# Moving the first layer's sums of squares to GpSimd and reordering the first loads and ScalarE's table load, in a two-layer streaming encoder

## The chip, the core and the metric

The kernel runs on one core of a Trainium2 chip. The metric is the device time of one execution in microseconds (us), the median of three runs. The core has five engines: TensorE (PE in the rows; PEld is its weight load), VectorE (DVE), ScalarE (ACT), GpSimd (POOL) and SyncE (SP). Each runs its own instructions in order. Here SP only issues transfers; ScalarE issues a few as well.

## The reference

One inference step of an encoder of two layers for 384 token rows: 256 of a prompt and 8 x 16 of running streams. Each layer normalises x, multiplies it by one wide input projection, runs sparse attention, a convolution and a pooling group on slices of the result, projects back to x, and adds a gated embedding. What the change touches is the first normalisation and the first products:

```python
def _rmsnorm(x, g):
    xf = x.astype(jnp.float32)
    y = xf * lax.rsqrt(jnp.mean(xf * xf, axis=-1, keepdims=True) + EPS) * g.astype(jnp.float32)
    return y.astype(x.dtype)

z = _split_cols(_rmsnorm(x, norm_mix) @ w_in)
```

with x of (384, 2048) and w_in of (2048, 6224) in float32.

## The kernel before

x lies in 16 tiles of 128 features by 384 tokens, x0 to x15. Every matmul is made of three: each operand is split in a high part (rounded by ScalarE's copy) and a low part (the remainder, by VectorE), and high by high, high by low and low by high are added up in a bank of TensorE's result memory (function mm3, lines 245 to 247). The normalisation is taken out of the products: TensorE multiplies the unscaled x, and the rows are scaled afterwards by rb, the reciprocal root of the mean square.

Weights come in pieces of up to 128 x 1024. For each piece SP issues the load (line 103, function w_dma, three raw buffers), ScalarE makes the high part whi (line 116), VectorE the low part wlo (line 117, function w_split, four buffers). The first six pieces belong to the first step (function first_step, line 862): 3, 3, 3, 3, 2 and 2 feature tiles with 336 columns each (keys of the indexer, its weights, and values), where x is the stationary operand. For every tile k line 185 makes xh, line 186 xl, and lines 877 to 879 issue nine matmuls of 336 columns, 144 in all. Piece 0 is loaded and split in three parts of one tile each. Behind it come 46 steps of 48 matmuls each (function mstep, 128 output features, two pieces), whose results are evacuated from the middle of the next step on; there are three banks ("mm") for them and five ("sd") for all else.

At the start VectorE writes a tile of ones, TensorE runs seven warm-up matmuls on it (line 282; each shows as two instructions), ScalarE issues the loads of 16 columns of constants (line 298) and of x0 to x2 (line 288), and SP issues piece 0, x3, x4, piece 1, x5 to x7, piece 2, x8 to x15. ScalarE's first arithmetic instruction brings the load of its function table (ACT_TABLE_LOAD).

The sum of squares of layer 0 goes along with the first step: for each x ScalarE squares it (lines 202, 206) and VectorE adds the square to ss (line 207; class SumSq). When the step of 48 matmuls behind the first step has been issued, the function stats issues three column sums on TensorE (line 174), the reciprocal root (lines 162 to 167), and, half a step later, the transposes that make rb (lines 179 and 182). The evacuations of the first step and of all later ones wait for rb.

The tile selh (eight 128 x 128 selection matrices, needed in the attention of the streams, much later) is loaded by SP in one transfer (line 349) right behind the first step's loads and converted to bfloat16 by ScalarE (line 350).

The order of the instructions on each engine is not exactly that of the program: at compile time a scheduler puts ready instructions first by its own estimates of their durations, and puts semaphores where one engine needs another's result. What it made of the program before is seen in the trace.

Of the kernel before, what the change touches and what calls it, by code (L numbers as in the profile page):

```python
# [11 lines left out]
AF = mybir.ActivationFunctionType  # L12
OP = mybir.AluOpType
# [4 lines left out]
KD = 16  # L18
TP = 256
NB = 8  # L20
# [23 lines left out]
FIRST = 336  # L44
# [7 lines left out]
def hybrid_kernel(ctx, tc, I, O):  # L52
    nc = tc.nc
    V, A, G, T, S = nc.vector, nc.scalar, nc.gpsimd, nc.tensor, nc.sync
# [37 lines left out]
    def parts(i, n):  # L92

        m = FIRST if i == 0 else n
        return [slice(c, c + m) for c in range(0, n, m)]

    def w_dma(upto):
        while st["dma"] < min(upto, len(pieces)):
            i = st["dma"]
            src, n = pieces[i]  # L100
            r = wpool.tile([128, 8 * 128], F32, name="wraw", tag="wraw", bufs=RAWS)
            for c in parts(i, n):
                S.dma_start(out=r[:, c], in_=src[:, c])
            raw[i] = r
            st["dma"] += 1

# [20 lines left out]
    def w_ahead():  # L127
        i = st["use"]
        w_split(i + PARTS - 1)
        w_dma(i + PARTS - 1 + RAWS)  # L130
# [9 lines left out]
    ones = const.tile([128, 128], F32, name="ones")  # L140
    identb = const.tile([128, 128], BF16, name="identb")
    selh = const.tile([128, NB, 128], BF16, name="selh")
# [6 lines left out]
    def tmp(shape=(128, N), name="t", bufs=6, dt=F32):  # L149
        return act.tile(list(shape), dt, name=name, tag="tmp" if name == "t" else name, bufs=bufs)  # L150

    def bank(tag):
        return psum.tile([128, 512], F32, name=tag, tag=tag, bufs=3 if tag == "mm" else 5)
# [16 lines left out]
    def stats(sumsq, n, out):  # L170

        ps = bank("sd")
        for i in range(3):
            T.matmul(ps[:, i:i + 1], sumsq.t[:, 128 * i:128 * i + 128], ones[:, 0:1], start=True, stop=True)
        y = rsqrt(ps[:, 0:3], n, 3)
        yield
        ps = bank("sd")
        for i in range(3):
            T.transpose(ps[:, 128 * i:128 * i + 128], y[:, i:i + 1].to_broadcast([128, 128]), ident)
        out["col"] = y  # L180
        out["rb"] = act.tile([128, N], F32, name="rb", tag="rb", bufs=2)
        V.tensor_copy(out["rb"], ps[:, :N])
# [9 lines left out]
    class SumSq:  # L192
# [3 lines left out]
            self.n = 0  # L196
            self.t = None

        def add(self, x, q=None):
            if self.t is None:  # L200
                self.t = act.tile([128, N], F32, name="ss", tag="ss", bufs=2)
                A.activation(self.t, x, AF.Square)
            else:
                if q is None:
                    q = tmp()
                A.activation(q, x, AF.Square)
                V.tensor_tensor(self.t, self.t, q, OP.add)

    def buf(which, part, k, name, dt=F32R):

        return act.tile([128, N], dt, name=name, tag=f"{which}{part}{k}", bufs=1)
# [28 lines left out]
    def run_pending(gate):  # L240
        while pending and gate():
            pending.popleft()()
# [6 lines left out]
    def mstep(xs, evac, gate, c0=0):  # L249

        ps = bank("mm")
        for h in range(2):
            w_ahead()
            hi, lo = w_next()
            for j in range(8):
                k = 8 * h + j
                mm3(ps[:, :N - c0], hi[:, 128 * j:128 * j + 128], lo[:, 128 * j:128 * j + 128], xs[k][0][:, c0:],
                    xs[k][1][:, c0:], k == 0, k == KD - 1)
            if h == 0:
                run_pending(gate)  # L260
            pump()
        pending.append(lambda: evac(ps))
# [15 lines left out]
    V.memset(ones, 1.0)  # L278

    warm = bank("sd")  # L280
    for _ in range(7):
        T.matmul(warm[:, :128], ones, ones, start=True, stop=True)
    xs, xt = [], []
    ss = SumSq()

    def x_in(k):
        x = buf("B", "hl"[k // 8], k % 8, f"x{k}", F32)
        (A if k < 3 else S).dma_start(out=x, in_=I["xT"][k])
        xt.append(x)

    def x_split(k):
# [3 lines left out]
        xs.append((hi, lo))  # L295

    x_dram = dram.tile([KD, 128, N], F32, name="x_dram")
    A.dma_start(out=cst[:, 384:400], in_=I["cst"][:, 384:400])
    for k in range(3):
        x_in(k)  # L300
    w_dma(1)
    for k in range(3, KD):
        x_in(k)
        if k in (4, 7):
            w_dma(2 if k == 4 else 3)

    def square_gen():
        for k in range(KD):
            q = buf("B", "hl"[k % 2], 8 + k // 2 % 2, f"sq{k}", F32)
            ss.add(xt[k], q)  # L310
            if k % 2:
                yield

    tracks.append(Track(square_gen()))


    for l in range(DEPTH):
# [4 lines left out]
        with ExitStack() as mixctx:  # L322
            mix = mixctx.enter_context(tc.tile_pool(name=f"mix{l}", bufs=1))

            def mt(shape, tag, bufs=1, dt=F32, name=None):
                return mix.tile(list(shape), dt, name=name or tag, tag=tag, bufs=bufs)
# [3 lines left out]
            def load_tab(i):  # L330
                tabs[i] = mt([128, 2, N], "tab", name=f"tab{i}")
                S.dma_start(out=tabs[i], in_=I["tab"][i])
# [7 lines left out]
            def loads():  # L340
                if l == 0:
                    S.dma_start(out=cst[:, 400:], in_=I["cst"][:, 400:])
                    S.dma_start(out=cst[:, :384], in_=I["cst"][:, :384])
                    V.tensor_copy(identb, ident)
                load_tab(0)
                S.dma_start(out=tabt, in_=I["tabt"])
                if l == 0:
                    t = mt([128, NB, 128], "qas", name="selhf")
                    S.dma_start(out=t, in_=I["selh"])
                    A.activation(selh, t, AF.Copy)  # L350

            if l > 0:
                loads()
# [5 lines left out]
            qas = mt([128, NB, 8, TS], "qas")  # L359
            q = [buf(oth, "l", 8 + h, f"q{l}_{h}", F32) for h in range(8)]  # L360
# [70 lines left out]
            def pre_ga(m):  # L431
                if m >= 2:
                    drain(lambda: f"conv{m - 2}" in flags)
                u = mt([128, 24, HALO + TS], "up", bufs=2, name="u")
                G.memset(u[:, 0, 0:30], 0.0)
                G.memset(u[:, 1, 0:14], 0.0)
                S.dma_start(out=u[:, 16:].rearrange("p b j -> p (b j)"), in_=I["cstate"][l, m])
                u_t[m] = u
# [473 lines left out]
            def pool_mm():  # L912
                hi, lo = w_next()
                for g in range(4):
                    ps = bank("sd")
                    c = slice(128 * g, 128 * g + 128)
                    mm3(ps[:, :N], hi[:, c], lo[:, c], r_t[g][0], r_t[g][1], True, True)
                    po[g] = buf(oth, "l", g, f"po{l}_{g}", F32)
                    A.activation(po[g], ps[:, :N], AF.Copy)

            def conv_mm():
                drain(lambda: "convy" in flags)
                w_ahead()
                a = w_next()
                b = w_next()
                ys = R["ys"]
                oc = []
                for m in range(4):
                    ps = bank("sd")
                    for k in range(4):  # L930
                        hi, lo = (a, b)[m // 2]
                        j = (4 * (m % 2) + k) * 128
                        mm3(ps[:, :N], hi[:, j:j + 128], lo[:, j:j + 128], ys[k][0], ys[k][1], k == 0, k == 3)
                    o = buf(oth, "l", 4 + m, f"oc{l}_{m}", F32)
                    A.activation(o, ps[:, :N], AF.Copy)
                    oc.append(o)
                R["oc"] = oc
# [7 lines left out]
            stat_track = stats(ss, D, R)  # L945
            first_step()
            if l == 0:
                loads()
            for n, (kind, i) in enumerate(ORDER):
                if n == POOL_AT:  # L950
                    pool_mm()
                if n == CONV_AT:
                    conv_mm()
                if kind == "ga":
                    pre_ga(i)
                mstep(xs, evs[kind](i), gate, CHUNK if kind == "qi" else 0)
                if l == 0 and n == 0:
                    next(stat_track)
                    tracks.append(Track(stat_track))
            run_pending(gate)  # L960


        with ExitStack() as xctx:
            xp = xctx.enter_context(tc.tile_pool(name=f"x{l}", bufs=1))
            x = []
            for k in range(KD):
                t = xp.tile([128, N], F32, name=f"xr{l}_{k}", tag=f"xr{k}")
# [4 lines left out]
            for k in range(2):  # L972
                t = tmp()
                S.dma_start(out=t, in_=I["pT"][l, :, k])
                split(t, phi[k], plo[k])
            ss = SumSq()
# [19 lines left out]
            stat_track = stats(ss, D, R2)  # L996
# [161 lines left out]
            ss = ss2  # L1158
# [136 lines left out]
```

## Time and profile before

| | us |
|---|---|
| median of three runs | 1503.79 |
| lowest, highest run | 1502.68, 1504.21 |
| the profiled execution's own time | 1504.57 |
| its span, first to last instruction | 1502.8 |
| TensorE busy | 1482.3 |
| VectorE busy | 981.7 |
| ScalarE busy | 666.9 |
| GpSimd busy | 6.4 |

The span starts with the first instruction of any engine; times in the rows count from there. "Busy" is the time in which an engine's instructions were under way. TensorE's matmuls overlap one another, so the distance between two starts, not the duration of one, tells its pace. "x14" behind an entry says how many instructions it holds, and the arrow in brackets says how long the engine was idle before it and what it waited for. The granted clock is 1.00 at 2.4 GHz and 0.50 at 1.2 GHz.

### The profile page before, as it was taken

The numbers are of one execution on the slowest core, as the hardware profiler recorded it, in microseconds if no ns is written. First come the engines' busy times: TensorE is split into PE (matmuls) and PEld (weight loads), VectorE is DVE, ScalarE is ACT, GpSimd is POOL, SyncE is SP. The second block draws the span as 40 slices with busy tenths as digits, with TensorE's granted clock in tenths as the row PEclk, the third lists the DMA queues.
The fourth block names the chain that finished last, engine by engine and source line by source line (L and its number), as shares of the span: only waits on it lengthen the run. The fifth ranks groups of instructions, "written<-read, shape, count | busy, mean of one in ns | idle before, by whom it ended". The sixth has DMA issues, their size and how long they took to land.

```text
span 1502.8 us, 22679 instructions
## 1 busy us (share of the span) xinstructions
PE 1482.3 (99%) x8832; PEld 1448.8 (96%) x8832; DVE 981.7 (65%) x1768; ACT 666.9 (44%) x1170; POOL 6.4 (0%) x40
## 2 busy tenths in 40 slices
PE   8999999999999999999999999999999999999996
PEld 8999999999999999999999999999999999999996
DVE  6778987975565444555549699978646554445554
ACT  7553424465443333444445433344644333345443
POOL 0000000000000000000000000000000000000000
PEclk9999999999999999999999999999999999999998
DMA  8554444334464444444454445443345444444332
GB/s 289 158 157 129 139 134 130 116 99 126 137 200 137 126 126 127 142 147 148 137 181 157 145 122 160 121 132 111 100 133 177 153 137 126 127 130 126 127 113 84
DMA packets 81435, 209.14 MB, mean 139 GB/s; under 512 B 11696, under 2 KB 37040, under 8 KB 81328
## 3 DMA queue, kind: packets, MB, share of 16 engines
q1 hardware_dynamic: 80464, 206.58, 44.1%
q8 instruction: 69, 1.13, 0.3%
q10 hardware_dynamic: 864, 1.12, 0.2%
q14 instruction: 38, 0.31, 0.1%
HBM read 196.90 MB, written 10.77 MB: 138 GB/s over the span
## 4 chain that ended last, share of the span: by engine, by line
PE 97%; DMA 1%; DVE 1%; ACT 0%; SPq 0%; issue 0%; DVEq 0%
PE mm L245 29%; PE mm L247 28%; PE mm L246 28%; PE sd L245 1%; PE sd L247 1%; PE sd L246 1%; PE sd L878 1%; PE sd L879 1%; PE sd L739 1%; PE sd L877 1%; PE sd L766 1%; DMA x<-in_xT_dram 1%; PE sd L672 1%; PE sd L709 1%; PE sd L801 0%; PE sd L827 0%
## 5 line engine op out<-in xcount | busy, mean ns | idle before, releaser
L116 ACT ACTIVATE whi<-wraw 128x1024 fp32r<-128x1024 f32 (+3 forms) x340 | 356.2, 1048 | 584.8 <-PE mm L246 420.7
L117 DVE TENSOR_TENSOR wlo<-wraw,whi 128x1024 fp32r<-128x1024 f32 (+3 forms) x340 | 411.0, 1209 | 228.5 <-ACT whi L116 223.3
L245 PE MATMUL mm<-xh,whi 128*128 128x384 f32 (+1 forms) x736 | 245.9, 334 | 0.0
L245 PE MATMUL mm<-nh,whi 128*128 128x384 f32 (+1 forms) x736 | 245.8, 334 | 0.0
L247 PE MATMUL mm<-nh,wlo 128*128 128x384 f32 (+1 forms) x736 | 244.8, 333 | 0.0
L247 PE MATMUL mm<-xh,wlo 128*128 128x384 f32 (+1 forms) x736 | 244.8, 333 | 0.0
L246 PE MATMUL mm<-nl,whi 128*128 128x384 f32 (+1 forms) x736 | 243.8, 331 | 0.0
L246 PE MATMUL mm<-xl,whi 128*128 128x384 f32 (+1 forms) x736 | 243.8, 331 | 0.0
L246 PE MATMUL mm<-cl,whi 128*128 128x384 f32 x512 | 171.0, 334 | 0.0
L247 PE MATMUL mm<-ch,wlo 128*128 128x384 f32 x512 | 171.0, 334 | 0.0
L245 PE MATMUL mm<-ch,whi 128*128 128x384 f32 x512 | 170.7, 334 | 0.0
L245 PE MATMUL mm<-ph,whi 128*128 128x384 f32 (+1 forms) x512 | 169.8, 332 | 0.0
L246 PE MATMUL mm<-pl,whi 128*128 128x384 f32 (+1 forms) x512 | 169.4, 331 | 0.0
L247 PE MATMUL mm<-ph,wlo 128*128 128x384 f32 (+1 forms) x512 | 169.4, 331 | 0.0
L468 DVE SCALAR_TENSOR_TENSOR ca<-u,cst,ca 128x384 f32<-128x384 f32 x240 | 146.9, 612 | 2.5
L245 PEld LDWEIGHTS mm<-xh,whi 128*128 128x128 f32 x736 | 138.2, 188 | 3.1 <-issue 1.8
L245 PEld LDWEIGHTS mm<-nh,whi 128*128 128x128 f32 x736 | 138.2, 188 | 3.1 <-issue 1.8
L247 PEld LDWEIGHTS mm<-xh,wlo 128*128 128x128 f32 x736 | 138.2, 188 | 1.6 <-issue 1.2
L247 PEld LDWEIGHTS mm<-nh,wlo 128*128 128x128 f32 x736 | 138.2, 188 | 1.6 <-issue 1.2
L246 PEld LDWEIGHTS mm<-xl,whi 128*128 128x128 f32 x736 | 138.2, 188 | 1.5 <-issue 1.0
L246 PEld LDWEIGHTS mm<-nl,whi 128*128 128x128 f32 x736 | 138.2, 188 | 1.5 <-issue 1.0
L246 PEld LDWEIGHTS mm<-pl,whi 128*128 128x128 f32 x512 | 96.2, 188 | 0.0
(274 smaller groups left out, 1877.0 us busy)
## 6 DMA issues: line engine op xcount, KB each, us to landing
wraw<-in_win_dram SPq DMA_DIRECT2D x184, 512.0 KB, 3.6
wraw<-in_wout_dram SPq DMA_DIRECT2D x64, 512.0 KB, 3.5
wraw<-in_wple_dram SPq DMA_DIRECT2D x64, 512.0 KB, 3.5
wraw<-in_wpp_dram SPq DMA_DIRECT2D x8, 512.0 KB, 3.5
wraw<-in_wfirst_dram SPq DMA_DIRECT2D x7, 504.0 KB, 3.8
xr<-in_xT_dram SPq DMA_DIRECT2D x16, 192.0 KB, 5.3
x_dram<-xr SPq DMA_DIRECT2D x16, 192.0 KB, 3.2
xr<-x_dram SPq DMA_DIRECT2D x16, 192.0 KB, 4.9
```

The source lines that it names most:

```text
L116: A.activation(hi[:, c], r[:, c], AF.Copy)
L117: V.tensor_tensor(lo[:, c], r[:, c], hi[:, c].bitcast(F32), OP.subtract)
L245: T.matmul(ps, hi_w, hx, start=first, stop=False)
L246: T.matmul(ps, hi_w, lx, start=False, stop=False)
L247: T.matmul(ps, lo_w, hx, start=False, stop=last)
L468: V.scalar_tensor_tensor(av, u[:, :, j:j + 16], w, av, OP.mult, OP.add)
L672: T.matmul(ps[j][:, :nk], qi[t + i][h, 64:192], kiT[h, :nk], start=True, stop=True)
L709: T.matmul(ps[j][:, :KS], qis[h, b + i].rearrange("p t j -> p (t j)"), kbs[i][h], start=True, stop=True)
L739: T.matmul(o, q[2 * hp + i][:, 128 * qt:128 * qt + 128], kT[g][:, :nk], start=True, stop=False)
L766: T.matmul(ps.rearrange("p (i c) -> p i c", i=4), Vt[:, kt, 128 * g:128 * g + 128], pt[:, kt], start=(kt == 0), stop=(kt == qt))
L877: T.matmul(outs[i], xh[:, c], wh, start=(k == 0), stop=False)
L878: T.matmul(outs[i], xh[:, c], wl, start=False, stop=False)
```

## The change

The diff has four parts. For layer 0 the squares of x0 to x11 and all additions to ss are made by GpSimd; the squares of x12 to x15 stay with ScalarE. ScalarE issues x0 first, then the 16 columns of constants, and then copies one column of the ones into column 128 of the bank that the warm-up matmuls write; there are eight of these instead of seven. x1, x2 and x3 are issued by SP, each behind one of the three parts of piece 0. selh is loaded and converted behind the fifth step of 48 matmuls, in two halves. Last, the column sums of layer 0 are no longer issued at the end of the first step of 48, but when the list of side tracks is stepped in the middle of the next one, and the transposes for rb at its end.

```diff
@@ -94,13 +94,15 @@
         m = FIRST if i == 0 else n
         return [slice(c, c + m) for c in range(0, n, m)]
 
-    def w_dma(upto):
+    def w_dma(upto, also=None):
         while st["dma"] < min(upto, len(pieces)):
             i = st["dma"]
             src, n = pieces[i]
             r = wpool.tile([128, 8 * 128], F32, name="wraw", tag="wraw", bufs=RAWS)
             for c in parts(i, n):
                 S.dma_start(out=r[:, c], in_=src[:, c])
+                if also is not None:
+                    also(c.start)
             raw[i] = r
             st["dma"] += 1
 
@@ -196,15 +198,22 @@
             self.n = 0
             self.t = None
 
-        def add(self, x, q=None):
+        def add(self, x, q=None, eng=None, sq=False):
+
+            def square(out):
+                if not sq:
+                    A.activation(out, x, AF.Square)
+                else:
+                    eng.tensor_tensor(out, x, x, OP.mult)
+
             if self.t is None:
                 self.t = act.tile([128, N], F32, name="ss", tag="ss", bufs=2)
-                A.activation(self.t, x, AF.Square)
+                square(self.t)
             else:
                 if q is None:
                     q = tmp()
-                A.activation(q, x, AF.Square)
-                V.tensor_tensor(self.t, self.t, q, OP.add)
+                square(q)
+                (eng or V).tensor_tensor(self.t, self.t, q, OP.add)
 
     def buf(which, part, k, name, dt=F32R):
 
@@ -278,14 +287,14 @@
     V.memset(ones, 1.0)
 
     warm = bank("sd")
-    for _ in range(7):
+    for _ in range(8):
         T.matmul(warm[:, :128], ones, ones, start=True, stop=True)
     xs, xt = [], []
     ss = SumSq()
 
     def x_in(k):
         x = buf("B", "hl"[k // 8], k % 8, f"x{k}", F32)
-        (A if k < 3 else S).dma_start(out=x, in_=I["xT"][k])
+        (A if k == 0 else S).dma_start(out=x, in_=I["xT"][k])
         xt.append(x)
 
     def x_split(k):
@@ -295,11 +304,11 @@
         xs.append((hi, lo))
 
     x_dram = dram.tile([KD, 128, N], F32, name="x_dram")
+    x_in(0)
     A.dma_start(out=cst[:, 384:400], in_=I["cst"][:, 384:400])
-    for k in range(3):
-        x_in(k)
-    w_dma(1)
-    for k in range(3, KD):
+    A.activation(warm[:, 128:129], ones[:, 0:1], AF.Copy)
+    w_dma(1, lambda c: x_in(c // FIRST + 1))
+    for k in range(4, KD):
         x_in(k)
         if k in (4, 7):
             w_dma(2 if k == 4 else 3)
@@ -307,7 +316,7 @@
     def square_gen():
         for k in range(KD):
             q = buf("B", "hl"[k % 2], 8 + k // 2 % 2, f"sq{k}", F32)
-            ss.add(xt[k], q)
+            ss.add(xt[k], q, G, k < 12)
             if k % 2:
                 yield
 
@@ -344,10 +353,6 @@
                     V.tensor_copy(identb, ident)
                 load_tab(0)
                 S.dma_start(out=tabt, in_=I["tabt"])
-                if l == 0:
-                    t = mt([128, NB, 128], "qas", name="selhf")
-                    S.dma_start(out=t, in_=I["selh"])
-                    A.activation(selh, t, AF.Copy)
 
             if l > 0:
                 loads()
@@ -955,8 +960,12 @@
                     pre_ga(i)
                 mstep(xs, evs[kind](i), gate, CHUNK if kind == "qi" else 0)
                 if l == 0 and n == 0:
-                    next(stat_track)
                     tracks.append(Track(stat_track))
+                if l == 0 and n == 4:
+                    for i in range(2):
+                        t = mt([128, 4, 128], "rp", bufs=2, name="selhf")
+                        S.dma_start(out=t, in_=I["selh"][:, 4 * i:4 * i + 4])
+                        A.activation(selh[:, 4 * i:4 * i + 4], t, AF.Copy)
             run_pending(gate)
```

## Rows read from the trace of the kernel before

**Rows 1.** The page's busy shares: us, share of the span, instructions

```profile
PE 1482.3 (99%) x8832; PEld 1448.8 (96%) x8832; DVE 981.7 (65%) x1768; ACT 666.9 (44%) x1170; POOL 6.4 (0%) x40
```

**Rows 2.** TensorE's waits over the span: line, releaser, us, times, longest

```profile
PE sd L877 <- ACT whi L116: 3.5, 2, 3.3
PE sd L878 <- DVE wlo L117: 1.8, 2, 1.5
```

**Rows 3.** Windows: stretch, length, busy us by engine, granted clock, DMA share, GB/s

```profile
7.70:12.62 4.92, 4.92 (x17) 4.92 (x18) 4.54 (x10) 4.92 (x12) 0.00 (x0) 1.00 1.04 380
12.62:23.40 10.78, 10.34 (x65) 9.79 (x64) 10.68 (x21) 10.78 (x21) 0.00 (x0) 1.00 1.06 384
23.40:26.36 2.96, 1.46 (x7) 1.17 (x8) 2.96 (x6) 2.96 (x6) 0.00 (x0) 1.00 0.27 82
26.36:29.72 3.36, 3.36 (x14) 3.36 (x13) 3.29 (x6) 1.94 (x4) 0.00 (x0) 0.50 0.89 272
```

**Rows 4.** Timeline of the beginning, ScalarE and SP: start, us, what; idle before

```profile
1.18 1.42 ACTq L288 DMA_DIRECT2D x<-in_xT_dram  x3
3.65 0.43 SPq L103 DMA_DIRECT2D wraw<-in_wfirst_dram  x1
5.36 1.28 ACT L185 ACT_TABLE_LOAD   x1 [5.36 <-DMA x<-in_xT_dram]
6.66 0.61 ACT L185 ACTIVATE xh<-x,cst 128x384 fp32r<-128x384 f32 x1
```

**Rows 5.** Timeline of TensorE in the first 37 us

```profile
1.05 3.36 PE L282 MATMUL sd<-ones 128*128 128x128 f32 x14 [1.05 <-DVE ones L278]
7.70 1.21 PE L877 MATMUL sd<-whi,xh 128*128 128x336 f32 x3 [3.29 <-ACT whi L116]
8.98 0.48 PE L879 MATMUL sd<-whi,xl 128*128 128x336 f32 x1
9.26 0.48 PE L878 MATMUL sd<-wlo,xh 128*128 128x336 f32 x1
...
26.64 0.48 PE L877 MATMUL sd<-whi,xh 128*128 128x336 f32 x1
26.92 0.48 PE L878 MATMUL sd<-wlo,xh 128*128 128x336 f32 x1
...
36.51 0.33 PE L245 MATMUL mm<-xh,whi 128*128 128x384 f32 x1
```

**Rows 6.** Groups of the first 37 us: line, shapes, count, busy us, mean ns

```profile
L186 DVE SCALAR_TENSOR_TENSOR xl<-x,cst,xh 128x384 fp32r<-128x384 f32 x16 | 9.4, 611 | 6.7 <-ACT xh L185 6.7
L207 DVE TENSOR_TENSOR ss<-ss,sq 128x384 f32<-128x384 f32 x15 | 8.3, 552 | 0.3
L206 ACT ACTIVATE sq<-x 128x384 f32<-128x384 f32 x15 | 7.6, 512 | 0.1
L117 DVE TENSOR_TENSOR wlo<-wraw,whi 128x1008 fp32r<-128x1008 f32 x3 | 3.6, 1199 | 0.0
```

**Rows 7.** Line 820: ns min/median/max, and what its engine sat idle for

```profile
L820 ACT ACTIVATE t<-sd x16: 269/277/278, 366.2 to 1146.6; 128x128 f32<-128x128 f32 x16
...
  PE sd L818: 17.8, 14
```

**Rows 8.** Line 1133, GpSimd's only arithmetic: ns min/median/max

```profile
L1133 POOL TENSOR_TENSOR xr<-xr,rbA x4: 724/727/732, 1488.9 to 1490.9; 128x256 f32<-128x256 f32 x4
```

**Rows 9.** Timeline from 44 to 53 us: column sums and scale row

```profile
44.83 0.72 PE L174 MATMUL sd<-ones,ss 128*128 128x1 f32 x6
...
52.03 0.55 DVE L182 COPY rb<-sd 128x384 f32<-128x384 f32 x1
```

**Rows 10.** Landings of weight pieces in the first 30 us

```profile
DMA to landing us min/median/max: 2.4/4.5/5.5
...
wraw<-in_wfirst_dram SPq DMA_DIRECT2D x3, 504.0 KB, 5.4
```

**Rows 11.** ScalarE's timeline near 25 us

```profile
25.14 1.05 ACT L350 ACTIVATE selh<-selhf 128x1024 bf16<-128x1024 f32 x1
```

## Prediction

> **What bounds the kernel now.** I read the page's busy shares first, then TensorE's waits, then the windows of the first 30 us, and last the order of events on each engine there. TensorE is busy in 99% of the span [rows 1], so nothing that only unloads another engine matters unless TensorE waited for it. Two lines account for its waits, but for the one ahead of the warm-ups, and all of them lie at the beginning [rows 2]: 3.3 us until the first converted weights came from ScalarE, and 1.5 us (and one short one) for a weight remainder from VectorE. From 36.5 us on it has work without a gap until the tail, which the change does not touch. So all that can be gained lies ahead of 36.5 us, where the first step (144 matmuls of 336 columns, lines 877 to 879) ends and the first matmul of the next step starts [rows 5].
>
> How long must that step take? Pairs of neighbouring starts give the pitch. At 8.98 and 9.26 us it is 0.28 us, and again at 26.64 and 26.92 us, where the clock column reads 0.50 [rows 3, 5]: that is 336 columns at 1.2 GHz. In between, from 12.62 to 23.40 us, 65 matmuls took 10.34 us, 0.159 each: 2.4 GHz. The clock column reads 1.00 in the first stage too, but the pitch says half. The 144 matmuls at 0.159 would take 22.9 us; from 7.70 to 36.51 us they took 28.8. The 5.9 us too many are the half clock at the start, the stall from 23.4 to 26.36 us (1.46 us busy in 2.96, with ScalarE and VectorE busy throughout [rows 3]), and the half clock behind the stall.
>
> **The change part by part.**
>
> *Start.* ScalarE now waits for x0, issued at 1.18 us and landed by 5.36, then loads its table for 1.28 us, then makes xh0 at 6.66, and TensorE starts at 7.70, 1.04 us behind xh0's start [rows 4, 5]. x0 moves to the slot 0.45 us earlier; with the same 4.18 us it lands at 4.9, and with the shortest landing of a first weight part, 2.4 us [rows 10], at 3.1. The table load moves off this path if it starts by 3.6 us. The copy that brings it writes one column of the bank that the warm-up matmuls write. Does it wait for them? The nearest row is a copy at line 820, which reads columns 0 to 127 of a bank and still waits for the later matmul at line 818, which writes columns 128 to 255 [rows 7]; so I take it that the copy waits for the last warm-up. 14 warm-up instructions took 3.36 us from 1.05 us on [rows 5]; 16 end at 4.9. I take the table load itself as running ahead of that wait and 0.2 us for a copy of one column (128 columns take 0.28 [rows 7]): xh0 at 5.1, TensorE at 6.15, a gain of 1.55 us. Bounds: 0.25 (table load behind the wait too: 4.9 + 1.28 + 0.2 = 6.4 instead of 6.66) and 2.8 (no wait and x0 at 3.1, where TensorE itself ends the warm-ups only at 4.9). The eighth warm-up matmul costs nothing as long as TensorE starts after 4.9. x1 and x2 go from ScalarE's queue to SP's and push piece 1 back by two issues, 0.9 us; the part on what is late next pays for that.
>
> *Clock at the start.* About 18 matmuls ran at 0.28 instead of 0.155: 2.2 us lost. The clock rose at 12.6 us, 4.9 us after the stream began and after a hole of 3.3 us behind the warm-ups. The hole would be 1.25 us. How much sooner the clock rises no row shows: between 0 and 2.2 us; I take 1.0.
>
> *Squares and sums on GpSimd.* ScalarE loses 12 squares of 0.51 us, 6.1 us, and VectorE 15 adds of 0.55, 8.3 us [rows 6]; ScalarE also loses the 1.05 us conversion at 25.14 us [rows 11]. In the 20 us in which both ran without a pause that is a third of their work, while the missing remainder came 1.5 us late. So the waits at 15.1, 23.4 and 25.6 us go, 2.0 us (1.8 on VectorE, 3.5 less 3.3 on ScalarE [rows 2]); lower bound 1.0. With the stall goes the fall of the clock behind it: 3.36 us at half clock is 1.5 us lost [rows 3]; lower bound 0.5, if a shorter stall comes back elsewhere. GpSimd gets 27 operations (12 squares, 15 adds). Its only row is a median of 0.727 us for 256 columns [rows 8]; for 384 that makes 1.09 by the columns, 0.73 if they counted for nothing: 27 of them are 29.4 or 19.7 us, and I take the 29.4. Begun at 4.9, the sum is ready at 34.3 us at most. Who needs it? The column sums at line 174, in TensorE's own order, at 44.83 us now [rows 9]; the change moves them half a step back. A step took 44.83 - 36.51 = 8.3 us, so that is 4.2 us. With a first step ended at about 31.5, they stand at 31.5 + 8.3 + 4.2 = 44 us: 10 us of slack, if GpSimd runs freely. The scale row rb, copied at 52.03 us now [rows 9], comes 4.2 us later in the order; the evacuations that wait for it free TensorE's three banks. TensorE waits nowhere behind it now [rows 2], so I cost this at 0; how much cover is left no row tells, and if it runs out, up to 4.2 us come on top, inside the range.
>
> *What is late next.* Weights: piece 1 was issued at 3.65 us [rows 4], in the new order near 4.5, and lands 5.4 us later [rows 10], at 9.9; with its conversion TensorE has it at 11. Its first 27 matmuls end between 10.3 (full clock) and 13.7 (half). I charge 1.0 us, bounds 0 and 2.0. The transfers ran at 380 GB/s all through that stretch [rows 3]; the constant selh (512 KB, 1.3 us of them) leaves it, which is why I charge no more. Its two halves, loaded and converted behind the fifth step, I cost at 0: from 26 us on TensorE waits for no conversion [rows 2].
>
> Sum: 1.55 + 1.0 + 2.0 + 1.5 - 1.0 = 5.05 us. The profiled execution took 1504.57 us, 1.77 more than its span; 1504.57 - 5.05 = 1499.5. The median of the runs lies 0.8 us below the profiled one, so 1503.8 - 5.05 gives **1498.8 us**. All upper ends give 8.5 us (2.8 + 2.2 + 2.0 + 1.5), 1495.3; all lower ones (0.25 + 0 + 1.0 + 0.5 - 2.0) give 1504.
>
> **The rivals.**
>
> *A, slower: GpSimd and VectorE shut each other out.* Nowhere in the trace does a GpSimd operation that reads SBUF run beside a VectorE operation with two SBUF inputs: in the tail, beside the four of [rows 8], VectorE reads one input from PSUM. In the first step nearly all of VectorE's work (lines 186 and 117) has two SBUF inputs, so this case is open. If only one of the two can run at a time, the work queues up: 29.4 us of GpSimd, 9.4 us of line 186, 16 x 336 columns at 1.2 us per 1008 of line 117, 6.4 us [rows 6], and some four later remainders of 1.2 us, 4.9 us, together 50 us from 4.9 on, so ready at 55 us. The sums are due at 44. Either TensorE stands 11 us at line 174, or it starves by as much in the first step: 1498.8 + 11 = 1510 us. It decides once GpSimd is held up by more than the 10 us of slack. For it: 15.8 us of VectorE's first step are of this kind. Against it: nothing that the trace shows.
> The Trainium skill states such a rule in "SBUF — State Buffer", section "SBUF: two separate sides": a VectorE operation with two SBUF inputs and a GpSimd operation that reads SBUF take a common pair of ports in turn, and the loser waits for the whole instruction. By that rule the time would be that of A; no run here shows it yet.
>
> *B, no difference: the start does not move and supply takes the rest.* The table load sits behind the warm-ups (gain 0.25), the clock rises no sooner, and the weights, which came at 380 GB/s already, hold TensorE where ScalarE and VectorE did: 0.25 + 2.0 + 1.5 - 2.0 = 1.8, 1502 us. For it: [rows 7] and the DMA column; against it: from 23.4 to 26.36 us the transfers nearly stopped (82 GB/s), so supply was not what held TensorE then.
>
> **How the numbers follow.** The forecast, gains of 3 us and more: 0.52. B: 0.14. A: 0.34; no row contradicts it and it would eat all gains. A change of under 0.2% (3 us) can hardly be told from none here. Faster by over 0.2% (below 1500.8) 0.52, within 0.14, slower (above 1506.8) 0.34. The likeliest case's own range is 1495.3 to 1501. The range that should hold 8 in 10 takes in B and most of A: 1496 to 1511.5.
>
> **What would show it.** Right: TensorE's first matmul near 6.2 us with the table load ahead of it, no wait at line 878 in the first step, no half clock near 27 us, the next step starting near 31.5 us, line 174 unwaited. A would show as GpSimd operations well above 1.1 us apart, VectorE's 0.61 and 1.20 us grown, and a wait at line 174 or 878. B would show as a first matmul near 7.4 us and ScalarE waiting for DMA on pieces 1 to 3. I am wrong if GpSimd's chain ends after 44 us.

## The result and the profile after

The median after is 1511.86 us (1510.99 to 1512.35) against 1503.24 us of the kernel before beside it: a ratio of 1.0058, 95% interval 1.0047 to 1.0070, so 8.6 us slower. The profiled execution took 1511.61 us, with a span of 1509.7 us, 6.9 us longer than before. The spans differ by less than the medians because the profiled execution of before, 1504.57 us, lies 1.3 us above its median; sums below that set one trace against the other account for the 7 us, not for the 8.6.

The page's span and busy shares, the lines that answer to [rows 1]:

```profile
span 1509.7 us, 22681 instructions
PE 1484.1 (98%) x8834; PEld 1450.5 (96%) x8834; DVE 989.5 (66%) x1753; ACT 662.9 (44%) x1160; POOL 41.0 (3%) x67
```

VectorE lost 15 additions (8.3 us by [rows 6]) and is busy 7.8 us longer. TensorE's waits (line, releaser, us, times, longest), answering to [rows 2]:

```profile
PE sd L883 <- DVE wlo L119: 9.7, 3, 6.7
PE sd L291 <- DVE ones L287: 1.1, 1, 1.1
PE sd L882 <- ACT xh L187: 0.8, 1, 0.8
```

(The second is the wait for the tile of ones ahead of the warm-ups; it was there before.) The 3.3 us ahead of the first matmul are 0.8 now, and nothing waits for whi. But the waits for a remainder, 1.8 us before, are 9.7. Line 883 is line 878 of before, 119 is 117, 188 is 186. TensorE's timeline (start, length, what; in brackets the idle time before it and what ended it), answering to [rows 5]:

```profile
1.05 3.78 PE L291 MATMUL sd<-ones 128*128 128x128 f32 x16 [1.05 <-DVE ones L287]
5.65 0.65 PE L882 MATMUL sd<-whi,xh 128*128 128x336 f32 x1 [0.81 <-ACT xh L187]
...
15.40 0.42 PE L883 MATMUL sd<-wlo,xh 128*128 128x336 f32 x1 [2.67 <-DVE wlo L119]
...
32.24 0.65 PE L883 MATMUL sd<-wlo,xh 128*128 128x336 f32 x1 [6.72 <-DVE wlo L119]
...
43.51 0.33 PE L254 MATMUL mm<-xh,whi 128*128 128x384 f32 x1
```

The first matmul starts 2.05 us sooner than before, the next step 7.0 us later. That is the difference of the spans, so all of the loss between the two profiled executions lies in the first step. The windows show what stood there (stretch, length, busy us by engine, granted clock, DMA share, GB/s), as [rows 3] do for before:

```profile
13.20:15.40 2.20, 0.00 (x1) 0.00 (x1) 2.20 (x3) 2.13 (x4) 2.20 (x2) 1.00 1.08 373
15.40:19.00 3.60, 3.60 (x15) 3.60 (x16) 3.60 (x4) 3.36 (x7) 3.60 (x4) 0.61 1.00 336
...
25.00:30.40 5.40, 0.53 (x4) 0.25 (x2) 5.40 (x6) 1.77 (x3) 5.32 (x6) 0.95 0.25 73
30.40:34.00 3.60, 1.76 (x6) 1.76 (x7) 3.60 (x3) 0.53 (x2) 3.44 (x3) 0.50 0.22 41
```

From 25.0 to 30.4 us TensorE (first column) has half a microsecond of work, ScalarE (fourth) a third of the time, the transfers move 73 GB/s, and VectorE and GpSimd (third and fifth) are busy with hardly a pause. Behind the stalls the clock column reads 0.61 and 0.50 (0.50 is 1.2 GHz).

The groups of the first 60 us (line, shapes, count, then busy us, mean ns of one, and idle before), answering to [rows 6]:

```profile
L216 POOL TENSOR_TENSOR ss<-ss,sq 128x384 f32<-128x384 f32 x15 | 20.9, 1390 | 0.5
L188 DVE SCALAR_TENSOR_TENSOR xl<-x,cst,xh 128x384 fp32r<-128x384 f32 x16 | 18.8, 1228 | 0.2 <-ACT xh L187 0.2
L207 POOL TENSOR_TENSOR sq<-x 128x384 f32<-128x384 f32 x11 | 13.6, 1238 | 0.1
L119 DVE TENSOR_TENSOR wlo<-wraw,whi 128x1008 fp32r<-128x1008 f32 x3 | 6.0, 2002 | 0.0
L353 DVE CAST identb<-cst 128x128 bf16<-128x128 f32 x1 | 1.0, 1024 | 0.0
L207 POOL TENSOR_TENSOR ss<-x 128x384 f32<-128x384 f32 x1 | 0.8, 825 | 3.1 <-DMA x<-in_xT_dram 3.1
```

The same xl took 611 ns before and takes 1228, the same remainder of 1008 columns 1199 and now 2002 [rows 6]. GpSimd's first square, made while VectorE had nothing to do, took 825 ns; the other squares and the additions took 1238 and 1390. VectorE's instructions are longer by 0.6 to 0.8 us, about one of GpSimd's. VectorE's and GpSimd's timelines around the long stall show it one by one:

```profile
20.69 9.58 DVE L188 SCALAR_TENSOR_TENSOR xl<-x,cst,xh 128x384 fp32r<-128x384 f32 x8
30.19 3.56 DVE L119 TENSOR_TENSOR wlo<-wraw,whi 128x1008 fp32r<-128x1008 f32 x2
...
22.70 1.14 POOL L207 TENSOR_TENSOR sq<-x 128x384 f32<-128x384 f32 x1
23.80 1.33 POOL L216 TENSOR_TENSOR ss<-ss,sq 128x384 f32<-128x384 f32 x1
...
28.55 10.84 POOL L216 TENSOR_TENSOR ss<-ss,sq 128x384 f32<-128x384 f32 x7
```

Eight xl take 9.58 us, 1.2 each, and GpSimd's instructions start 1.1 and 1.3 us apart: one of the one, one of the other. The fourth piece's remainder stands behind those eight on VectorE, starts at 30.19 us and frees TensorE at 32.24. Its high part had been ready since 19.64 us (18.60 + 1.04), as ScalarE's timeline shows together with the start:

```profile
1.66 1.28 ACT L118 ACT_TABLE_LOAD   x1 [1.66 <-PEq L1275]
4.00 0.48 ACT L118 ACTIVATE whi<-wraw 128x336 fp32r<-128x336 f32 x1 [1.06 <-DMA wraw<-in_wfirst_dram]
4.98 1.12 ACT L187 ACTIVATE xh<-x,cst 128x384 fp32r<-128x384 f32 x2 [0.50 <-DMA cst<-in_cst_dram]
...
6.38 0.15 ACT L309 ACTIVATE sd<-ones 128x1 f32<-128x1 f32 x1
...
18.60 1.04 ACT L118 ACTIVATE whi<-wraw 128x1008 fp32r<-128x1008 f32 x1 [0.24 <-DMA wraw<-in_wfirst_dram]
```

The result of GpSimd's chain itself, the sum, is ready at 39.4 us (28.55 + 10.84), and the column sums that need it stand at 55.99 us in TensorE's order and wait for nothing.

### The profile page after: what moved, and what is told of

Same layout as the page of the kernel before. It is cut to its first block, busy times and chain, and to the rows that moved or that the text cites. A ratio compares the mean times of both kernels' runs of the same rounds, so it can differ in the third digit from the quotient of the medians.

```text
span 1509.7 us, 22681 instructions
## 1 busy us (share of the span) xinstructions
PE 1484.1 (98%) x8834; PEld 1450.5 (96%) x8834; DVE 989.5 (66%) x1753; ACT 662.9 (44%) x1160; POOL 41.0 (3%) x67
## 4 chain that ended last, share of the span: by engine, by line
PE 97%; DVE 1%; DMA 1%; ACT 0%; SPq 0%; issue 0%; DVEq 0%; ACTq 0%
PE mm L254 28%; PE mm L256 28%; PE mm L255 28%; PE sd L254 1%; PE sd L256 1%; PE sd L255 1%; PE sd L883 1%; PE sd L884 1%; DMA wraw<-in_wfirst_dram 1%; PE sd L744 1%; PE sd L882 1%; PE sd L771 1%; PE sd L677 1%; DVE xl L188 1%; PE sd L714 1%; PE sd L806 0%
## 5 line engine op out<-in xcount | busy, mean ns | idle before, releaser
L119 DVE TENSOR_TENSOR wlo<-wraw,whi 128x1024 fp32r<-128x1024 f32 (+3 forms) x340 | 416.5, 1225 | 233.5 <-ACT whi L118 231.2
```

The lines of the kernel that those rows point to most:

```text
L119: V.tensor_tensor(lo[:, c], r[:, c], hi[:, c].bitcast(F32), OP.subtract)
```

## The experiments

The theory behind the first runs was Rival A: GpSimd's operations lengthen VectorE's, and the remainders come late. Against it stood that the new order of VectorE's instructions is to blame (the fourth remainder behind eight xl), or the other three parts of the change. The trace of before answers part of this by itself: there, too, the fourth remainder stood behind eight xl, of 0.6 us each:

```profile
19.08 1.67 DVE L186 SCALAR_TENSOR_TENSOR xl<-x,cst,xh 128x384 fp32r<-128x384 f32 x3
...
21.14 1.14 DVE L186 SCALAR_TENSOR_TENSOR xl<-x,cst,xh 128x384 fp32r<-128x384 f32 x2
...
22.33 0.61 DVE L186 SCALAR_TENSOR_TENSOR xl<-x,cst,xh 128x384 fp32r<-128x384 f32 x1
...
23.33 1.14 DVE L186 SCALAR_TENSOR_TENSOR xl<-x,cst,xh 128x384 fp32r<-128x384 f32 x2
24.39 1.20 DVE L117 TENSOR_TENSOR wlo<-wraw,whi 128x1008 fp32r<-128x1008 f32 x1
```

So that place in the queue is not new, and the expectations that call it so are wrong in this.

Every time is given with its ratio to the kernel before, timed on the same chip, and the ratio's 95% interval; a difference between two experiments can be one between two chips. The line numbers of one and the same instruction differ by a few from run to run; the names of the tiles are the same.

**The change without GpSimd's part.** The sums come back to ScalarE and VectorE, all else as changed.

```diff
-            ss.add(xt[k], q, G, k < 12)
+            ss.add(xt[k], q)
```

> The changed kernel with its squares back on ScalarE and its sums back on VectorE; the other three parts of the change stay, and behind the first step TensorE's order is the same. Exclusion theory (a VectorE operation with two SBUF inputs and a GpSimd operation that reads SBUF run one after the other): line 188 falls from 1.23 back to 0.61 us and the 1008-column remainder from 2.00 to 1.20; the waits at line 883 (9.7 us now) fall under 4 us; 1498 to 1503 us. Order theory (the remainder of the fourth piece is queued behind eight xl now, and the loads come later, whatever GpSimd does): this order is kept, so the wait of 6.7 us stays and the time is 1508 to 1512.

Measured: 1502.98 us against 1502.81, ratio 0.9999 (0.999 to 1.0008). The 8.6 us are gone. The fourth remainder still comes behind the same eight xl, so that order alone does not cost them; TensorE's waits for remainders are 1.2 us instead of 9.7. The groups:

```profile
L188 DVE SCALAR_TENSOR_TENSOR xl<-x,cst,xh 128x384 fp32r<-128x384 f32 x16 | 9.5, 616 | 0.0
L119 DVE TENSOR_TENSOR wlo<-wraw,whi 128x1008 fp32r<-128x1008 f32 x3 | 3.6, 1206 | 0.5 <-ACT whi L118 0.5
```

VectorE's durations are those of before. The first matmul starts at 5.79 us, 1.9 us sooner than before, but TensorE then waits 1.3 us at 22.04 and 1.2 us at 24.01 with half clock behind it: the other parts together are worth nothing that this measurement tells from none as long as the sums are made in the first step.

**GpSimd's part alone.** The kernel before, with only the squares and additions on GpSimd.

```diff
...
-            ss.add(xt[k], q)
+            ss.add(xt[k], q, G, k < 12)
```

> The kernel before with only the squares and sums moved to GpSimd; loads, table load, warm-ups and selh as before. Exclusion theory: VectorE's two-input operations double as in the changed kernel, TensorE waits 8 us or more for remainders, 1509 to 1515 us (worse than the changed kernel, as the earlier start is missing). Order theory: with the loads in their old order 1502 to 1504.

Measured: 1513.89 us, ratio 1.0073 (1.0056 to 1.0089), 11.1 us slower than before. The waits:

```profile
PE sd L885 <- DVE wlo L117: 9.3, 3, 6.7
PE sd L884 <- ACT whi L116: 3.3, 1, 3.3
```

The same long wait of 6.7 us, beside the old start of 3.3; xl took 1209 ns and the 1008-column remainder 2000. So the part that costs is this one, with the old loads and the old start too.

**No sums at all.** The squares and sums of x1 to x15 are left out, on every engine.

```diff
-            q = buf("B", "hl"[k % 2], 8 + k // 2 % 2, f"sq{k}", F32)
-            ss.add(xt[k], q, G, k < 12)
+            q = None
+            if k == 0:
+                ss.add(xt[k], q)
```

> The changed kernel without the sum of squares of x1 to x15 (the scale rows come from x0 alone): neither GpSimd nor ScalarE nor VectorE makes them. Exclusion theory: this is the case that the forecast's sum described, VectorE at 0.61 and 1.20 us, no wait over 1 us at line 883, 1496 to 1499 us. Order theory: 1506 or more, as the eight xl are still queued ahead of the fourth remainder.

Measured: 1499.27 us, ratio 0.9974 (0.9964 to 0.9983): 3.5 us faster than before. This is close to the prediction's own case, sums that disturb nobody. TensorE's only wait behind the warm-ups, and the window from the clock's rise to the end of the first step:

```profile
PE sd L883 <- ACT xh L187: 0.7, 1, 0.7
```

```profile
12.06:31.99 19.93, 19.93 (x130) 19.91 (x130) 13.12 (x23) 10.71 (x18) 0.00 (x0) 1.00 0.82 298
```

No stall and no half clock behind one; the next step starts at 31.99 us, where 31.5 was forecast. The order changed too: the six column-sum instructions ran at 7.42 us, inside the first step, and up to 12.06 us the matmuls ran at a pitch of 0.28 us, 1.2 GHz.

**Half the columns.** GpSimd's operations take 192 of the 384 columns, but for the first; the rest of the sum is left out.

```diff
...
-                    eng.tensor_tensor(out, x, x, OP.mult)
+                    m = N if out is self.t else n
+                    eng.tensor_tensor(out[:, :m], x[:, :m], x[:, :m], OP.mult)
...
-                (eng or V).tensor_tensor(self.t, self.t, q, OP.add)
+                (eng or V).tensor_tensor(self.t[:, :n], self.t[:, :n], q[:, :n], OP.add)
...
```

> The changed kernel with GpSimd's operations (all but the first square) on 192 of the 384 columns; the rest of the sum is left out. Their number and order stay. Exclusion theory: a VectorE operation waits for one GpSimd operation of half the length, line 188 near 0.90 to 1.0 us instead of 1.23, TensorE's waits at line 883 about half of 9.7 us, 1502 to 1507 us. If the number of GpSimd's instructions or their semaphores were what slows VectorE, line 188 stays at 1.2 us and the time at 1511 to 1513.

Measured: 1509.04 us, ratio 1.004 (1.0025 to 1.0055). The durations answered to the number of columns:

```profile
L189 DVE SCALAR_TENSOR_TENSOR xl<-x,cst,xh 128x384 fp32r<-128x384 f32 x16 | 13.3, 882 | 0.1
L120 DVE TENSOR_TENSOR wlo<-wraw,whi 128x1008 fp32r<-128x1008 f32 x3 | 4.3, 1437 | 1.6 <-ACT whi L119 1.6
```

xl is 0.27 us above its own 0.611, where whole columns put 0.62 on it. The time was missed (1502 to 1507 expected). The order had changed: the column sums moved into the first step, to 28.35 us, and the waits are others.

```profile
PE sd L884 <- ACT whi L119: 3.5, 1, 3.5
PE sd L177 <- POOL ss L218: 2.4, 1, 2.4
```

The second is the other form of Rival A, TensorE standing at the column sums (line 174 of before) for GpSimd's chain. So this run shows that VectorE's durations follow the length of GpSimd's operations, and nothing on how the time goes with it.

**GpSimd busy without reading.** The sums left out as above, and 64 memsets of 384 columns that nobody reads.

```diff
-            ss.add(xt[k], q, G, k < 12)
+            for _ in range(4):
+                G.memset(q, 0.0)
+            if k == 0:
+                ss.add(xt[k])
```

> The kernel of e3 (no sums but x0's) with 64 memsets of 128 x 384 on GpSimd that nobody reads: GpSimd is busy for some 25 to 30 us of the beginning, but it reads nothing from SBUF. If only a GpSimd operation that reads SBUF shuts VectorE out: line 188 stays at 0.61 us and the time at e3's, 1498 to 1500.5. If any GpSimd operation on SBUF does: line 188 near 1.0 us or more and 1504 or more.

Measured: 1499.62 us, ratio 0.9971 (0.996 to 0.9982), as without the memsets. They filled GpSimd until 23.9 us:

```profile
L320 POOL MEMSET sq<- 128x384 f32 x64 | 22.9, 416 | 0.3 <-POOLq L1278 0.3
L188 DVE SCALAR_TENSOR_TENSOR xl<-x,cst,xh 128x384 fp32r<-128x384 f32 x16 | 8.9, 609 | 0.5 <-ACT xh L187 0.5
```

A GpSimd busy with writing alone does not lengthen VectorE's two-input operations; one busy with the squares and additions, which read two operands from SBUF, does. No run has a GpSimd operation with one operand.

**Only the additions on GpSimd.** All squares on ScalarE.

```diff
-            ss.add(xt[k], q, G, k < 12)
+            ss.add(xt[k], q, G)
```

> The changed kernel with all squares on ScalarE; only the 15 sums are GpSimd's. TensorE's order is that of the changed kernel. Exclusion theory: 15 instead of 27 GpSimd operations stand in VectorE's way in the first step; each takes 0.6 us or so from VectorE, so some 7 of the 16 us come back, TensorE's waits at line 883 fall from 9.7 to 2 to 5 us, 1503 to 1508 us. If only the length of GpSimd's chain mattered: no wait at the column sums before, so no change, 1511 to 1513.

Measured: 1509.90 us, ratio 1.0043 (1.0028 to 1.0058): a miss. With 15 instead of 27 operations the longest wait for a remainder was 6.3 us instead of 6.7. VectorE's and GpSimd's timelines tell why:

```profile
19.05 9.04 DVE L188 SCALAR_TENSOR_TENSOR xl<-x,cst,xh 128x384 fp32r<-128x384 f32 x7
...
12.65 15.03 POOL L216 TENSOR_TENSOR ss<-ss,sq 128x384 f32<-128x384 f32 x11 [0.88 <-ACT sq L205]
```

Eleven additions, once they no longer had to wait for ScalarE's squares, ran without a pause from 12.65 to 27.68 us, and so beside seven of the eight xl that stand ahead of the fourth remainder, 1.29 us each. Here it counted less how many operations GpSimd had than beside which of VectorE's they fell. The additions read ss and sq, not x, so it is not the reading of one and the same tile that lengthens xl.

**The fourth remainder ahead of the last four xl.** GpSimd's work unchanged; xl12 to xl15 are put behind the fourth piece's remainder.

```diff
...
+        if k >= 12:
+            with tc.issue_after(st["fourth"]):
+                split_scaled(xt[k], vec(0, NM + k), hi, lo)
...
```

> The changed kernel with one order more: VectorE makes the remainder of the fourth weight piece ahead of xl12 to xl15 instead of behind them; all of GpSimd's work stays. If exclusion costs its time through what is queued ahead of that remainder: four xl of 1.2 us come out of the 6.7 us wait, which falls to 2 us or so (a later wait of 1 to 2 us for xl12 or the fifth remainder may appear), and the half clock behind it may go, 1505 to 1508 us. If VectorE's lost 16 us have to be paid wherever they lie, the wait only moves: 1510 to 1512.

Measured: 1507.16 us, ratio 1.0024 (1.0014 to 1.0034). The waits for remainders fell from 9.7 to 6.4 us, with the longest 2.7:

```profile
PE sd L889 <- DVE wlo L119: 6.4, 4, 2.7
```

The place in VectorE's queue made some 4.7 of the lost microseconds (1511.86 - 1507.16, on two chips); the rest, 4.2 us against the kernel before on the same chip (1502.92), is still there, and xl still takes 1240 ns. The whole loss needs both: instructions that have become twice as long, which is new, and an order, as it was before, that puts eight of them ahead of an urgent one.

**The sums behind the first step's splits.** No GpSimd; squares and additions on ScalarE and VectorE, but placed behind the split of the first step's last piece.

```diff
...
-            ss.add(xt[k], q, G, k < 12)
-            if k % 2:
+            a, v = st["behind"]
+            with tc.issue_after(a), tc.issue_after(v):
+                ss.add(xt[k], q)
+            if k in (5, 11):
...
```

> The changed kernel, complete, without GpSimd: ScalarE squares, VectorE adds, but all of them ordered behind the split of the first step's last weight piece. Exclusion theory: the first step runs as in the kernel without sums (next step starts near 32 us, no wait over 1 us), and ScalarE and VectorE have idle time for 8 us of sums each behind it: 1498 to 1500.5 us, faster than the kernel before. If the sums only move the stall: a wait of 2 us or more at lines 245 to 247 or at the column sums, 1501.5 to 1505.

Measured: 1498.66 us, ratio 0.997 (0.9959 to 0.9981), faster than both kernels. The next step starts at 30.61 us. Its waits:

```profile
PE sd L885 <- ACT whi L118: 1.7, 1, 1.7
...
PE sd L886 <- DVE wlo L119: 0.5, 1, 0.5
```

What the change wanted, the sums out of the first step's way, was to be had by moving them in time instead of to another engine. The 1.7 and 0.5 us end at 11.74 and 12.98 us; they are for piece 1 of the weights, on which ScalarE could begin at 10.64 us.

**The same with the beginning of before.** The kernel before, its sums and column sums placed as in the last one.

```diff
...
-            ss.add(xt[k], q)
-            if k % 2:
+            a, v = st["behind"]
+            with tc.issue_after(a), tc.issue_after(v):
+                ss.add(xt[k], q)
+            if k in (5, 11):
...
-                    next(stat_track)
```

> The kernel before (old order of loads, table load behind x0, selh early, seven warm-ups) with its sums on ScalarE and VectorE ordered behind the split of the first step's last piece and the column sums half a step later, as in e5. What it differs by from e5 is the new beginning alone: first matmul near 7.7 instead of 5.6 us. If the beginning is worth what it starts earlier: 1500 to 1501.5 us, 2 us above e5's 1498.7. If transfers set the pace of the first step: 1498.5 to 1499.5, as e5.

Measured: 1499.86 us, ratio 0.9977 (0.9968 to 0.9987), with the first matmul at 6.94 us and the next step at 31.75. The later sums alone are worth 3.1 us (1502.92 - 1499.86); with the new beginning and the later load of selh, by which the two kernels differ too, it is 4.4 (1503.10 - 1498.66). The rest, 1.2 us (1499.86 - 1498.66), lies between what the two theories expected, on two chips; I don't call it settled. With the same order of loads as before, x0 was awaited until 4.61 us here and until 5.36 in the trace of before [rows 4], so that part of an earlier first matmul can be the spread of single executions.

**No copy.** The kernel without GpSimd's part, without the copy into the warm-up bank and with seven warm-up matmuls.

```diff
-    for _ in range(8):
+    for _ in range(7):
...
-    A.activation(warm[:, 128:129], ones[:, 0:1], AF.Copy)
...
-            ss.add(xt[k], q, G, k < 12)
+            ss.add(xt[k], q)
```

> The kernel of e1 (changed, sums on ScalarE and VectorE) without the copy of a constant and with seven warm-ups instead of eight. If the copy brings the table load forward, the load falls back behind the wait for x0 and TensorE's first matmul comes at 6.5 us or later, 1503.5 to 1506. If the new order of the first instructions brings it (ScalarE's first one waits for one transfer only), the load stays at 1.7 us, the first matmul near 5.8, and the time at 1501.5 to 1504.5, the same as e1.

Measured: 1502.44 us, ratio 0.9996 (0.9987 to 1.0005), against 0.9999 with the copy. ScalarE's timeline:

```profile
1.66 1.28 ACT L118 ACT_TABLE_LOAD   x1 [1.66 <-PEq L1274]
```

The table load comes at the same time without the copy, ahead of the first conversion of weights (line 118), and the first matmul at 5.78 us, against 5.79. The copy brings nothing here.

**The loads of x1 to x3 in ScalarE's queue.** The kernel with the later sums, and three loads moved back from SP's queue.

```diff
-        (A if k == 0 else S).dma_start(out=x, in_=I["xT"][k])
+        (A if k < 4 else S).dma_start(out=x, in_=I["xT"][k])
```

> The kernel with the sums on ScalarE and VectorE behind the first step's splits, but with the loads of x1, x2 and x3 in ScalarE's queue behind x0's and the constant's, as x1 and x2 were before, instead of SyncE's. It asks what the term on supply in the prediction (1.0 us, bounds 0 and 2.0) was worth: with the three loads out of SyncE's queue, piece 1 of the weights is issued 1.4 us sooner (4.57 to about 3.2 us). If supply by issue order holds TensorE there, the waits of 1.7 and 0.5 us for piece 1 shrink to 1 us or less together and the time is 0.5 to 1.2 us below 1498.7. If the transfers' bandwidth sets the landing of piece 1, the waits stay near 2 us and the time stays within 0.4 us of 1498.7. If ScalarE's three extra issues (0.45 us each, ahead of its table load) delay the first split, the first matmul moves from 5.6 to 6 to 7 us and the time rises by up to 1.3 us.

Measured: 1500.05 us, ratio 0.9979 (0.997 to 0.9988), 1.4 us above the kernel that it is made from. ScalarE's timeline and TensorE's:

```profile
1.66 2.63 ACTq L299 DMA_DIRECT2D x<-in_xT_dram  x3
4.38 1.28 ACT L311 ACT_TABLE_LOAD   x1 [4.38 <-DMA wraw<-in_wfirst_dram]
...
7.32 0.72 PE L885 MATMUL sd<-whi,xh 128*128 128x336 f32 x3 [2.48 <-ACT whi L118]
```

The last of the three expectations came, a little beyond its figures: behind its three issues the table load, which the copy (line 311) brings here, starts at 4.38 instead of 1.66 us and the first matmul at 7.32 instead of 5.64. Piece 1 was no longer waited for, issued at 4.14 instead of 4.57 us (3.2 was expected) and with a later start; that gave back 2.2 us. But some 11 matmuls from 9.12 us on ran at a pitch of 0.28 us, 1.4 us more, and the next step started at 31.39 us, 0.8 later.

## Why the prediction was wrong

The direction was wrong; what came is Rival A, whose time was 1510 us and whose mechanism the experiments bear out.

**The step that failed** is the one on squares and sums, and in it the words "if GpSimd runs freely": GpSimd's 27 operations were costed as its own time, ready at 34.3 us, and VectorE's xl and remainders were left at their rows of before. The trace shows 0.611 turned into 1.228 us and 1.199 into 2.002, and the waits that were to shrink by 2.0 us grew to 9.7. The half clock that was to give back 1.5 us came twice: about 11 matmuls behind the stall at 15.4 us and 14 behind the one at 32.24 ran at a pitch of 0.28 instead of 0.155 us, 3.1 us. Against before that makes: start -2.05, clock at the start about -0.6 (some 13 instead of 18 matmuls at half clock, at 0.125 us each), waits behind the start from 2.0 to 9.7, +7.7, half clock behind stalls from 1.5 to 3.1, +1.6. Together +6.65 us, where the next step started 7.0 us later.

The forecast was given 0.52 although no row stood for it: the prediction said itself that nowhere in the trace does a reading GpSimd operation run beside a two-input VectorE operation. Without a row for the pair, "beside" was an assumption, and it held up all of the gain. The Trainium skill had the rule ("SBUF — State Buffer", section "SBUF: two separate sides"): whichever of such a pair starts first has the common ports for its whole instruction, and the other waits. The trace agrees in the turns, with 1.2 us for each of the eight xl of 9.58 us beside one GpSimd operation; it differs in the length of the wait, which was some 0.6 us and not the 0.825 of GpSimd's operation alone, and there the measurement decides. It agrees too in the exception that the page makes, since writing memsets left xl at 0.609 us.

**Where Rival A was off.** It held GpSimd's chain up to 55 us and let it decide from 10 us of slack on. The chain ended at 39.4 us, earlier than the 44 us that the prediction named as the point where it would be wrong, and the column sums, at 55.99 us behind a later first step, waited for nothing. The damage was done on the other side of the pair, to VectorE's remainders and so at line 883; Rival A had named that as its other form, at the same price. The 9.7 us of waits that came against the 11 us that it charged is a near hit from a sum that was wrong in its parts: an operation of GpSimd alone took 0.825 us, not 1.09, and its chain ended 16 us earlier than charged. That the time came so near is luck in the sum; the mechanism is not.

**The start** was mis-sized the safe way: first matmul at 5.65 us, forecast 6.15. x0 had landed by 4.26 us, where GpSimd's first square starts; xh0 followed at 4.98, after 0.50 us of waiting for the 16 columns of constants, which are now issued behind x0. But the mechanism was another: the copy, taken to bring the table load, ran at 6.38 us, behind xh0, and the run without it has the load at 1.66 us all the same. With only the loads of x0 and the constants ahead of it in ScalarE's queue, the first conversion of weights now comes first, and the table load runs ahead of that, at 1.66 us, while before it ran behind the wait for x0, at 5.36; what decides this no run shows. The run with three loads put back gave 1.7 us of the start away.

**The clock at the start** (1.0, bounds 0 and 2.2) was worth about 0.6 in the changed kernel. In the kernel with later sums TensorE ran at a pitch of 0.155 us, 2.4 GHz, from its second matmul on, so the upper bound is real; in the kernel without sums some 18 matmuls ran at 0.28, as before, so the lower bound is real too. What decides between these was not found.

**Supply** (1.0, bounds 0 and 2.0) cost nothing in the changed kernel, whose first stall was for a remainder of VectorE's. Where the clock was up from the start it took back 2.2 us (1.7 and 0.5), a little above the bound and as much as the clock had given.

**The sum itself**, 5.05 us, can be set against the kernels that keep their sums off the path: 3.5 us with no sums, 4.4 with later ones. So the total was right in sign and a little large for sums that lengthen nothing; for the single terms this shows little, since some were too small and some too large. With the sums still in the first step the new beginning gave nothing measurable (0.9999), although the profiled first step ended 1.66 us sooner (34.85 against 36.51). The two profiled executions differ by about as much, 1504.57 and 1503.06 us, while the medians do not: the one of before was longer than its median, that without GpSimd's part was not.

## What to carry to other kernels

Cost an operation moved to an idle engine as free only if a row of the trace shows that engine and its neighbour at work on the same kinds of operands at once, each at its own duration; if no such row exists, cost the pair as one queue and look for what is urgent in the neighbour's. In these runs two-input VectorE work on SBUF and reading GpSimd work were such a queue. To take work off a critical stretch, first ask whether it can be done later on the engine that has it: alone that gave 3.1 us here and the other engine cost 11.1; with the rest of the change it was 4.4 gained and 8.6 lost.

## What the runs showed of the hardware

VectorE and GpSimd, each with a full queue, took turns one for one: 1.2 us for an xl of 0.61, and a GpSimd operation of 0.825 us alone cost the pair only some 0.6.

A one-input conversion on VectorE from SBUF to SBUF suffers too: 128 columns took 0.218 us in the kernel before, 1.024 beside GpSimd's sums, 0.614 beside those of half the columns. Beside the memsets, which left the two-input operations alone, it took 1.787 us, from 22.22 to 24.01 us, and the last memset was over at 23.92 (2.92 + 21.00):

```profile
22.22 1.79 DVE L356 CAST identb<-cst 128x128 bf16<-128x128 f32 x1
...
2.92 21.00 POOL L320 MEMSET sq<- 128x384 f32 x59
```

So it seems not to have got its turn between two memsets. It is one instruction, no run here tested it by itself, and VectorE's next one, the copy that makes rb, is recorded from 23.48 us on, ahead of the conversion's end, so that its exact end is not sure. The Trainium skill ("SBUF — State Buffer", section "SBUF: two separate sides") lists, beside two-input operations, VectorE operations in a mode that uses both ports, and sets these against any GpSimd operation; this row agrees if the conversion is one of them, which no row shows.
